# Binary cross-entropy: from three pools and casting stores to one in-place float32 ring with a clip

## Chip, cores and metric

One core of a Trainium2 chip. The metric is the device time of one execution in microseconds (us), as a median over runs. The program runs on one core alone; all runs quoted are of the state "fast". The profile shows one execution from its first to its last instruction, some 1.7 us less than the timed value.

## The reference

Two inputs of 8192 x 8192 float32 (predictions, uniform in 0.01 to 0.99, and targets, 0 or 1), one float32 output of the same shape:

```python
pred = np.clip(pred, eps, 1 - eps)                                   # eps = 1e-7
return -(target * np.log(pred) + (1 - target) * np.log(1 - pred))
```

As the targets are 0 or 1, this is `-log(|target - 1 + pred|)`: one subtraction, an absolute value (or square), one logarithm, one scaling. Each input is read once and the output written once: 805.3 MB on the HBM side.

## The kernel before

The rows are cut into 64 blocks of 128 rows, 128 partitions x 32 KiB. Targets are cast to bf16 on the way in; the result is kept as fp16 and cast back to float32 on the way out. Three pools with 3, 2 and 2 buffers carry predictions, targets and results.

```python
pool_p = ctx.enter_context(tc.tile_pool(name="bce_p", bufs=3 if big else 2))
pool_t = ctx.enter_context(tc.tile_pool(name="bce_t", bufs=2))
pool_o = ctx.enter_context(tc.tile_pool(name="bce_o", bufs=2))
# ...
def ops(bi, rows, r0, g0, t_p, t_t):
    t_o = pool_o.tile([P, F], fp16, name="t_o", tag="t_o")
    p_sl = t_p[:rows]
    nc.vector.scalar_tensor_tensor(out=p_sl, in0=p_sl, scalar=1.0, in1=t_t[:rows], op0=sub, op1=add)
    nc.scalar.activation(out=p_sl, in_=p_sl, func=Square)
    nc.scalar.activation(out=p_sl, in_=p_sl, func=Ln)
    nc.vector.tensor_scalar(out=t_o[:rows], in0=p_sl, scalar1=-0.5, scalar2=None, op0=mult)
    # ... the store of t_o is noted as pending
for bi in range(n_blk):
    # ... predictions (SyncE for block 0, else GpSimd), then targets (GpSimd), then the store of block bi-2 (GpSimd)
    # ... ops(); the last two blocks in 4 and 8 column pieces, in place in float32, stored from SyncE
```

Of the kernel before, what the change touches and what calls it, by code (L numbers as in the profile page):

```python
# [1 line left out]

# [4 lines left out]


@with_exitstack
def kernel(  # L10
    ctx: ExitStack,
    tc: tile.TileContext,
    pred: bass.AP,
    target: bass.AP,
    out: bass.AP,
):
    nc = tc.nc
    fp32 = mybir.dt.float32
    fp16 = mybir.dt.float16
    bf16 = mybir.dt.bfloat16  # L20

    P = nc.NUM_PARTITIONS

    pred_f = pred.flatten_outer_dims()
    target_f = target.flatten_outer_dims()
    out_f = out.flatten_outer_dims()

    R, C = pred_f.shape

    F = 8192 if C % 8192 == 0 else C  # L30
    n_col = C // F
    n_row = (R + P - 1) // P
    n_blk = n_row * n_col

    big = (R % P == 0) and n_blk >= 8 and F == 8192

    sub = mybir.AluOpType.subtract
    add = mybir.AluOpType.add
    mult = mybir.AluOpType.mult

    Square = mybir.ActivationFunctionType.Square
    Ln = mybir.ActivationFunctionType.Ln

    pool_p = ctx.enter_context(tc.tile_pool(name="bce_p", bufs=3 if big else 2))
    pool_t = ctx.enter_context(tc.tile_pool(name="bce_t", bufs=2))
    pool_o = ctx.enter_context(tc.tile_pool(name="bce_o", bufs=2))
    pool_w = ctx.enter_context(tc.tile_pool(name="bce_w", bufs=1))

    warm = pool_w.tile([1, 8], fp32, name="warm", tag="warm")
    nc.vector.memset(warm, 1.0)  # L50
    nc.scalar.activation(out=warm, in_=warm, func=Ln)  # L51

    lb = n_blk - 1
    slb = n_blk - 2

    pending: dict[int, list] = {}

    def emit_store(b: int, n: int | None = None):
        lst = pending[b]
        n = len(lst) if n is None else n  # L60
        for _ in range(n):
            dram, sl = lst.pop(0)
            nc.gpsimd.dma_start(out=dram, in_=sl)  # L63
        if not lst:
            del pending[b]

    def ops(bi, rows, r0, g0, t_p, t_t):
        t_o = pool_o.tile([P, F], fp16, name="t_o", tag="t_o")
        p_sl = t_p[:rows]
        nc.vector.scalar_tensor_tensor(  # L70
            out=p_sl, in0=p_sl, scalar=1.0, in1=t_t[:rows], op0=sub, op1=add
        )
        nc.scalar.activation(out=p_sl, in_=p_sl, func=Square)  # L73
        nc.scalar.activation(out=p_sl, in_=p_sl, func=Ln)  # L74
        nc.vector.tensor_scalar(  # L75
            out=t_o[:rows], in0=p_sl, scalar1=-0.5, scalar2=None, op0=mult
        )
        pending.setdefault(bi, []).append(
            (out_f[r0 : r0 + rows, g0 : g0 + F], t_o[:rows])
        )  # L80

    def ops_tail(rows, r0, g0, t_p, t_t, nchunk):
        W = F // nchunk
        for k in range(nchunk):
            c0 = k * W
            p_sl = t_p[:rows, c0 : c0 + W]
            nc.vector.scalar_tensor_tensor(  # L87
                out=p_sl,
                in0=p_sl,
                scalar=1.0,  # L90
                in1=t_t[:rows, c0 : c0 + W],
                op0=sub,
                op1=add,
            )
            nc.scalar.activation(out=p_sl, in_=p_sl, func=Square)  # L95
            nc.scalar.activation(out=p_sl, in_=p_sl, func=Ln)  # L96
            nc.vector.tensor_scalar(  # L97
                out=p_sl, in0=p_sl, scalar1=-0.5, scalar2=None, op0=mult
            )
            nc.sync.dma_start(  # L100
                out=out_f[r0 : r0 + rows, g0 + c0 : g0 + c0 + W], in_=p_sl
            )

    for bi in range(n_blk):
        i, j = divmod(bi, n_col)
        r0 = i * P
        rows = min(P, R - r0)
        g0 = j * F

        t_p = pool_p.tile([P, F], fp32, name="t_p", tag="t_p")  # L110
        t_t = pool_t.tile([P, F], bf16 if big else fp32, name="t_t", tag="t_t")

        if big and bi == 0:
            nc.sync.dma_start(out=t_p[:rows], in_=pred_f[r0 : r0 + rows, g0 : g0 + F])
        else:
            nc.gpsimd.dma_start(out=t_p[:rows], in_=pred_f[r0 : r0 + rows, g0 : g0 + F])  # L116
        nc.gpsimd.dma_start(out=t_t[:rows], in_=target_f[r0 : r0 + rows, g0 : g0 + F])  # L117

        s = bi - 2
        if s in pending:  # L120
            emit_store(s)

        if big and bi == slb:
            ops_tail(rows, r0, g0, t_p, t_t, 4)
        elif big and bi == lb:
            ops_tail(rows, r0, g0, t_p, t_t, 8)
        else:
            ops(bi, rows, r0, g0, t_p, t_t)

    for b in sorted(pending):  # L130
        emit_store(b)


# [1 line left out]
_INS = ['pred', 'target']  # L135
_OUTS = [((8192, 8192), 'float32')]


# [23 lines left out]
```

## Time and profile before

| | before |
|---|---|
| median (3 runs) | 1867.4 us (1867.38 to 1867.8) |
| span of the profile | 1865.7 us |
| Vector / Scalar busy | 45% / 48% |
| DMA engines | 9 or 10 tenths in all 40 slices |
| steady distance between blocks (600 to 1750 us) | 29.06 us |

The prediction below shows the lines and reads them.

Some measures come from the packet and landing records of the trace rather than from a printed view. A 4 MB transfer is spread over 16 DMA engines, each with eight row packets. A row packet normally takes 1.21 to 1.25 us. Each engine reports its own landing; the **landing spread** is the time from the first to the last of the 16 landings of one DMA. The **end of the last targets** is when the last packet of the last target load ends.

### The profile page before, as it was taken

To read this page: it belongs to the slowest core of one execution; us is meant where nothing else is said; L and a number is where in the kernel's file an instruction comes from. 1 tells how busy PE (TensorE), PEld (TensorE's weight loads), DVE (VectorE), ACT (ScalarE), POOL (GpSimd) and SP (SyncE) were. 2 spreads that over 40 slices of the span, in tenths; PEclk is the share of its full clock that TensorE was granted. 3 is DMA by queue.
4 is the path that set the end of the run, shared out by engine and by line. 5 is a ranking of instruction groups with operands and counts; after the bars stand their busy time and mean duration, and the time that the engine had idled before them with its cause. 6 is when DMAs were issued, how large, how long until landed. Compare 5 with 4: busy or idle time off the path is not lost.

```text
span 1865.7 us, 804 instructions
## 1 busy us (share of the span) xinstructions
DVE 841.3 (45%) x149; ACT 903.3 (48%) x150; POOL 100.9 (5%) x193
## 2 busy tenths in 40 slices
DVE  2645344453443534435344353453534535345353
ACT  3653644535445354453544635446354463553654
POOL 0000000000000000000000000000000000000000
DMA  9999999999999999999999999999999999999999
GB/s 325 338 377 353 351 379 344 375 356 347 384 341 376 356 346 387 344 368 363 343 388 345 364 369 341 390 344 360 371 343 386 344 359 372 347 379 352 352 378 351
DMA packets 29093, 671.14 MB, mean 360 GB/s; under 512 B 3232, under 2 KB 3232, under 8 KB 4256
## 3 DMA queue, kind: packets, MB, share of 16 engines
q0 software_dynamic: 27216, 658.52, 99.9%
q1 hardware_dynamic: 1872, 12.58, 1.7%
q14 instruction: 5, 0.04, 0.0%
HBM read 536.87 MB, written 268.44 MB: 432 GB/s over the span
## 4 chain that ended last, share of the span: by engine, by line
DMA 80%; issue 14%; ACT 2%; DVE 2%; another core or an unknown queue 1%; POOL 0%; POOLq 0%; DVEq 0%; PEldq 0%
DMA t_t<-in_target_dram 80%; DVE t_p L70 1%; ACT t_p L96 1%; ACT t_p L95 1%; DVE t_o L75 0%; ACT t_p L73 0%; ACT t_p L74 0%; DVE t_p L87 0%; DVE t_p L97 0%; POOL t_p L116 0%; POOL out_dram L63 0%; POOLq L117 0%; POOL t_t L117 0%; POOLq L63 0%
## 5 line engine op out<-in xcount | busy, mean ns | idle before, releaser
L73 ACT ACTIVATE t_p<-t_p 128x8192 f32<-128x8192 f32 x62 | 435.8, 7029 | 923.6 <-DVE t_p L70 923.6
L75 DVE TENSOR_SCALAR t_o<-t_p 128x8192 f16<-128x8192 f32 x62 | 274.4, 4427 | 845.0 <-ACT t_p L74 845.0
L70 DVE SCALAR_TENSOR_TENSOR t_p<-t_p,t_t 128x8192 f32<-128x8192 f32 x62 | 538.9, 8693 | 144.8 <-DMA t_t<-in_target_dram 144.8
L74 ACT ACTIVATE t_p<-t_p 128x8192 f32<-128x8192 f32 x62 | 435.8, 7029 | 2.0
L63 POOL DMA_DIRECT2D out_dram<-t_o x62 | 33.4, 538 | 1121.9 <-DVE t_o L75 1101.2
L117 POOL DMA_DIRECT2D t_t<-in_target_dram x64 | 34.1, 533 | 581.5 <-DVE t_p L70 580.7
L116 POOL DMA_DIRECT2D t_p<-in_pred_dram x63 | 33.9, 537 | 0.3 <-issue 0.3
L95 ACT ACTIVATE t_p<-t_p 128x1024 f32<-128x1024 f32 (+1 forms) x12 | 15.6, 1327 | 26.5 <-DVE t_p L87 26.5
L87 DVE SCALAR_TENSOR_TENSOR t_p<-t_p,t_t 128x1024 f32<-128x1024 f32 (+1 forms) x12 | 18.4, 1575 | 17.2 <-DMA t_t<-in_target_dram 17.2
L96 ACT ACTIVATE t_p<-t_p 128x1024 f32<-128x1024 f32 (+1 forms) x12 | 15.6, 1330 | 0.1
L97 DVE TENSOR_SCALAR t_p<-t_p 128x1024 f32<-128x1024 f32 (+1 forms) x12 | 10.3, 868 | 7.9 <-ACT t_p L96 7.9
L51 ACT ACT_TABLE_LOAD x1 | 1.3, 1283 | 0.7 <-PEq L146 0.7
L50 DVE MEMSET warm<- 1x8 f32 x1 | 0.1, 65 | 0.8 <-PEq L146 0.8
L51 ACT ACTIVATE warm<-warm 1x8 f32<-1x8 f32 x1 | 0.2, 208 | 0.0
L146 POOL MEMSET const-float32-0.0<- 128x1 f32 x1 | 0.1, 100 | 0.2 <-issue 0.2
L146 POOL MEMSET const-bfloat16-1.0<- 128x1 bf16 x1 | 0.1, 102 | 0.0
L146 POOL MEMSET const-float32-1.0<- 128x1 f32 x1 | 0.1, 100 | 0.0
L146 POOL MEMSET const-uint8-127<- 128x1 uint8 x1 | 0.1, 100 | 0.0
## 6 DMA issues: line engine op xcount, KB each, us to landing
t_p<-in_pred_dram POOLq DMA_DIRECT2D x63, 4096.0 KB, 49.3
out_dram<-t_o POOLq DMA_DIRECT2D x62, 4096.0 KB, 40.1
t_t<-in_target_dram POOLq DMA_DIRECT2D x64, 2048.0 KB, 49.0
t_p<-in_pred_dram SPq DMA_DIRECT2D x1, 4096.0 KB, 19.6
out_dram<-t_p SPq DMA_DIRECT2D x4, 1024.0 KB, 27.3
out_dram<-t_p SPq DMA_DIRECT2D x8, 512.0 KB, 8.5
```

The source lines that it names most:

```text
L51: nc.scalar.activation(out=warm, in_=warm, func=Ln)
L63: nc.gpsimd.dma_start(out=dram, in_=sl)
L70: nc.vector.scalar_tensor_tensor(out=p_sl, in0=p_sl, scalar=1.0, in1=t_t[:rows], op0=sub, op1=add)
L73: nc.scalar.activation(out=p_sl, in_=p_sl, func=Square)
L74: nc.scalar.activation(out=p_sl, in_=p_sl, func=Ln)
L75: nc.vector.tensor_scalar(out=t_o[:rows], in0=p_sl, scalar1=-0.5, scalar2=None, op0=mult)
L87: nc.vector.scalar_tensor_tensor(out=p_sl, in0=p_sl, scalar=1.0, in1=t_t[:rows, c0 : c0 + W], op0=sub, op1=add,)
L95: nc.scalar.activation(out=p_sl, in_=p_sl, func=Square)
L96: nc.scalar.activation(out=p_sl, in_=p_sl, func=Ln)
L97: nc.vector.tensor_scalar(out=p_sl, in0=p_sl, scalar1=-0.5, scalar2=None, op0=mult)
L116: nc.gpsimd.dma_start(out=t_p[:rows], in_=pred_f[r0 : r0 + rows, g0 : g0 + F])
L117: nc.gpsimd.dma_start(out=t_t[:rows], in_=target_f[r0 : r0 + rows, g0 : g0 + F])
```

## The change

The stated intent: one ring of four 32 KiB slots for predictions, worked in place in float32 to the end, and a matching ring of targets; a clip as in the reference; and one GpSimd queue in the order store, predictions, targets, so that a load waits for a store issued one block earlier. The diff is condensed; cuts are marked.

```diff
-    pool_p (3 buffers), pool_t (2), pool_o (2)                  [cut]
+    ring_p = pool.tile([P, SLOTS * W], fp32, ...)               # SLOTS = 4, W = 8192
+    ring_t = pool.tile([P, SLOTS * W], bf16, ...)
-        t_o = pool_o.tile([P, F], fp16, ...)                    # result in fp16, casting store
+    def clip(k, ...):   tensor_scalar(out=p, in0=p, scalar1=EPS, scalar2=1 - EPS, max, min)
+    def front(k, ...):  scalar_tensor_tensor(out=p, in0=t, scalar=1.0, in1=p, subtract, add)
+                        activation(out=p, in_=p, func=Act.Abs)   # was Square
+                        activation(out=p, in_=p, func=Act.Ln)
+    def back(k, ...):   tensor_scalar(out=p, in0=p, scalar1=-1.0, mult)   # was -0.5, to fp16
+        for k in range(SLOTS):
+            load(k)
+        clip(0)
+        front(0)
+        for k in range(1, n - 1):
+            clip(k)
+            front(k)
+            back(k - 1)
+            store(k - 1)                                         # plain float32
+            if k >= 2 and k - 2 + SLOTS < n:
+                load(k - 2 + SLOTS)                              # slot of block k-2
+        back(n - 2)
+        store(n - 2)                                             # last two blocks: SyncE
+        clip(n - 1)                                              # then half, quarter, quarter
+        [cut: front, back and two half-width stores of the last block]
```

More of the change, by code (lines that the diff above doesn't have):

```diff
@@ L4 @@
 import concourse.tile as tile
-from concourse import bass_utils, mybir
+from concourse import mybir
 from concourse._compat import with_exitstack
+EPS = 1e-7
+W = 8192
+SLOTS = 4
 @with_exitstack
@@ L18 @@
     fp32 = mybir.dt.float32
-    fp16 = mybir.dt.float16
     bf16 = mybir.dt.bfloat16
+    Alu = mybir.AluOpType
+    Act = mybir.ActivationFunctionType
     P = nc.NUM_PARTITIONS
-    pred_f = pred.flatten_outer_dims()
-    target_f = target.flatten_outer_dims()
-    out_f = out.flatten_outer_dims()
-    R, C = pred_f.shape
-    F = 8192 if C % 8192 == 0 else C
-    n_col = C // F
-    n_row = (R + P - 1) // P
-    n_blk = n_row * n_col
-    big = (R % P == 0) and n_blk >= 8 and F == 8192
-    sub = mybir.AluOpType.subtract
@@ L38 @@
-    add = mybir.AluOpType.add
-    mult = mybir.AluOpType.mult
-    Square = mybir.ActivationFunctionType.Square
-    Ln = mybir.ActivationFunctionType.Ln
-    pool_p = ctx.enter_context(tc.tile_pool(name="bce_p", bufs=3 if big else 2))
-    pool_t = ctx.enter_context(tc.tile_pool(name="bce_t", bufs=2))
-    pool_o = ctx.enter_context(tc.tile_pool(name="bce_o", bufs=2))
-    pool_w = ctx.enter_context(tc.tile_pool(name="bce_w", bufs=1))
-    warm = pool_w.tile([1, 8], fp32, name="warm", tag="warm")
@@ L50 @@
-    nc.vector.memset(warm, 1.0)
-    nc.scalar.activation(out=warm, in_=warm, func=Ln)
-    lb = n_blk - 1
-    slb = n_blk - 2
-    pending: dict[int, list] = {}
-    def emit_store(b: int, n: int | None = None):
-        lst = pending[b]
-        n = len(lst) if n is None else n
-        for _ in range(n):
-            dram, sl = lst.pop(0)
-            nc.gpsimd.dma_start(out=dram, in_=sl)
-        if not lst:
-            del pending[b]
-    def ops(bi, rows, r0, g0, t_p, t_t):
-        t_o = pool_o.tile([P, F], fp16, name="t_o", tag="t_o")
-        p_sl = t_p[:rows]
+    R, C = pred.shape
@@ new lines, with chunks @@
+    n = R * C // (P * W)
+    assert n * P * W == R * C and n > SLOTS
+    def chunks(ap):
+        return ap.rearrange("r c -> (r c)").rearrange("(k p w) -> k p w", p=P, w=W)
+    pred_c, target_c, out_c = chunks(pred), chunks(target), chunks(out)
+    pool = ctx.enter_context(tc.tile_pool(name="rings", bufs=1))
+    ring_p = pool.tile([P, SLOTS * W], fp32, name="ring_p", tag="ring_p")
+    ring_t = pool.tile([P, SLOTS * W], bf16, name="ring_t", tag="ring_t")
+    warm = pool.tile([1, 8], fp32, name="warm", tag="warm")
@@ new lines, in slot, with load, store, clip @@
+    def slot(ring, k, off=0, w=W):
+        c = k % SLOTS * W + off
+        return ring[:, c : c + w]
+    def load(k):
+        queue = nc.sync if k == 0 else nc.gpsimd
+        queue.dma_start(out=slot(ring_p, k), in_=pred_c[k])
+        nc.gpsimd.dma_start(out=slot(ring_t, k), in_=target_c[k])
+    def store(k, off=0, w=W):
+        queue = nc.sync if k >= n - 2 else nc.gpsimd
+        queue.dma_start(out=out_c[k, :, off : off + w], in_=slot(ring_p, k, off, w))
+    def clip(k, off=0, w=W):
+        p = slot(ring_p, k, off, w)
+        nc.vector.tensor_scalar(
+            out=p, in0=p, scalar1=EPS, scalar2=1 - EPS, op0=Alu.max, op1=Alu.min
+        )
@@ L70, in ops, with front @@
+    def front(k, off=0, w=W):
+        p, t = slot(ring_p, k, off, w), slot(ring_t, k, off, w)
         nc.vector.scalar_tensor_tensor(
-            out=p_sl, in0=p_sl, scalar=1.0, in1=t_t[:rows], op0=sub, op1=add
+            out=p, in0=t, scalar=1.0, in1=p, op0=Alu.subtract, op1=Alu.add
         )
-        nc.scalar.activation(out=p_sl, in_=p_sl, func=Square)
-        nc.scalar.activation(out=p_sl, in_=p_sl, func=Ln)
-        nc.vector.tensor_scalar(
-            out=t_o[:rows], in0=p_sl, scalar1=-0.5, scalar2=None, op0=mult
-        )
@@ L78, in ops @@
-        pending.setdefault(bi, []).append(
-            (out_f[r0 : r0 + rows, g0 : g0 + F], t_o[:rows])
-        )
-    def ops_tail(rows, r0, g0, t_p, t_t, nchunk):
-        W = F // nchunk
-        for k in range(nchunk):
-            c0 = k * W
-            p_sl = t_p[:rows, c0 : c0 + W]
-            nc.vector.scalar_tensor_tensor(
-                out=p_sl,
-                in0=p_sl,
-                scalar=1.0,
-                in1=t_t[:rows, c0 : c0 + W],
-                op0=sub,
-                op1=add,
-            )
-            nc.scalar.activation(out=p_sl, in_=p_sl, func=Square)
-            nc.scalar.activation(out=p_sl, in_=p_sl, func=Ln)
-            nc.vector.tensor_scalar(
-                out=p_sl, in0=p_sl, scalar1=-0.5, scalar2=None, op0=mult
-            )
-            nc.sync.dma_start(
-                out=out_f[r0 : r0 + rows, g0 + c0 : g0 + c0 + W], in_=p_sl
-            )
@@ L104 @@
-    for bi in range(n_blk):
-        i, j = divmod(bi, n_col)
-        r0 = i * P
-        rows = min(P, R - r0)
-        g0 = j * F
-        t_p = pool_p.tile([P, F], fp32, name="t_p", tag="t_p")
-        t_t = pool_t.tile([P, F], bf16 if big else fp32, name="t_t", tag="t_t")
-        if big and bi == 0:
-            nc.sync.dma_start(out=t_p[:rows], in_=pred_f[r0 : r0 + rows, g0 : g0 + F])
-        else:
-            nc.gpsimd.dma_start(out=t_p[:rows], in_=pred_f[r0 : r0 + rows, g0 : g0 + F])
-        nc.gpsimd.dma_start(out=t_t[:rows], in_=target_f[r0 : r0 + rows, g0 : g0 + F])
-        s = bi - 2
-        if s in pending:
-            emit_store(s)
-        if big and bi == slb:
-            ops_tail(rows, r0, g0, t_p, t_t, 4)
-        elif big and bi == lb:
-            ops_tail(rows, r0, g0, t_p, t_t, 8)
-        else:
-            ops(bi, rows, r0, g0, t_p, t_t)
@@ L130, with back @@
-    for b in sorted(pending):
-        emit_store(b)
+        nc.scalar.activation(out=p, in_=p, func=Act.Abs)
+        nc.scalar.activation(out=p, in_=p, func=Act.Ln)
+    def back(k, off=0, w=W):
+        p = slot(ring_p, k, off, w)
+        nc.vector.tensor_scalar(out=p, in0=p, scalar1=-1.0, scalar2=None, op0=Alu.mult)
+    with tc.manual_schedule():
+        for k in range(SLOTS):
+            load(k)
+        nc.vector.memset(warm, 1.0)
+        nc.scalar.activation(out=warm, in_=warm, func=Act.Ln)
+        clip(0)
[9 more added lines that the diff above has]
+        store(n - 2)
+        h, q = W // 2, W // 4
+        clip(n - 1)
+        front(n - 1, 0, h)
+        front(n - 1, h, q)
+        back(n - 1, 0, h)
+        store(n - 1, 0, h)
+        front(n - 1, h + q, q)
+        back(n - 1, h, q)
+        back(n - 1, h + q, q)
+        store(n - 1, h, h)
```

## The prediction

> **What bounds the kernel now.** I start with the page's totals, because they say whether an engine or the transfers set the time.
>
> ```profile
> span 1865.7 us, 804 instructions
> DVE 841.3 (45%) x149; ACT 903.3 (48%) x150; POOL 100.9 (5%) x193
> DMA  9999999999999999999999999999999999999999
> q0 software_dynamic: 27216, 658.52, 99.9%
> HBM read 536.87 MB, written 268.44 MB: 432 GB/s over the span
> ```
>
> No compute engine is busy half the time, while the DMA engines are full in every slice and the GpSimd queue alone accounts for 99.9% of their time. The last line is the important one: 536.87 + 268.44 = 805.3 MB cross the HBM side, three transfers of 4.19 MB for each of 64 blocks. A target transfer lands as 2 MB of bf16 but is read as 4 MB of float32.
>
> Second view: how one block runs in the steady state, in order of time (start, duration, engine, line, wait before it).
>
> ```profile
> 903.15 0.54 POOL L63 DMA_DIRECT2D out_dram<-t_o  x1 [18.05 <-DVE t_o L75]
> 903.68 0.54 POOL L116 DMA_DIRECT2D t_p<-in_pred_dram  x1
> 904.73 8.69 DVE L70 SCALAR_TENSOR_TENSOR t_p<-t_p,t_t 128x8192 f32<-128x8192 f32 x1 [1.87 <-DMA t_t<-in_target_dram]
> 913.46 7.03 ACT L73 ACTIVATE t_p<-t_p 128x8192 f32<-128x8192 f32 x1 [15.06 <-DVE t_p L70]
> 913.72 0.53 POOL L117 DMA_DIRECT2D t_t<-in_target_dram  x1 [9.50 <-DVE t_p L70]
> 920.51 7.03 ACT L74 ACTIVATE t_p<-t_p 128x8192 f32<-128x8192 f32 x1
> 927.58 4.43 DVE L75 TENSOR_SCALAR t_o<-t_p 128x8192 f16<-128x8192 f32 x1 [14.15 <-ACT t_p L74]
> 933.74 8.69 DVE L70 SCALAR_TENSOR_TENSOR t_p<-t_p,t_t 128x8192 f32<-128x8192 f32 x1 [1.74 <-DMA t_t<-in_target_dram]
> ```
>
> Two successive L70 start at 904.73 and 933.74, 29.01 us apart; over many blocks I get 29.05. In that period Vector works 13.1 us and Scalar 14.1 us. 12.58 MB in 29.05 us is 433 GB/s.
>
> Third view: the issues, with the time from issue to landing.
>
> ```profile
> t_p<-in_pred_dram POOLq DMA_DIRECT2D x63, 4096.0 KB, 49.3
> out_dram<-t_o POOLq DMA_DIRECT2D x62, 4096.0 KB, 40.1
> t_t<-in_target_dram POOLq DMA_DIRECT2D x64, 2048.0 KB, 49.0
> ```
>
> A transfer needs about 29.05 / 3 = 9.68 us of the DMA engines, yet it lands 40 to 49 us after issue: four or five stand in line. So the chain of waits, which repeats "target DMA 49 us, then 9 us" (a two-buffer wait), describes the line, not a latency that could be removed. The packet records confirm it. In the steady state the target phase lasts 9.65 us, the store phase 9.68 us and the prediction phase 9.71 us, although two of these cast and one does not. The casts therefore cost no rate now.
>
> **What the Trainium skill says.** "DMA: Bandwidth & Descriptors", section "Where 436 GB/s comes from", puts the ceiling of the 16 DMA engines at 435.2 GB/s. This trace's 433 is within 0.5% of it, so by an estimate from that page 805.3 MB cannot take less than 1850.5 us, and all that any reordering can save is 15 us (0.8%). The same page's "SWDGE vs HWDGE vs iDMA" says that a casting transfer has to be issued from GpSimd. That is why target loads stay there; the float32 stores no longer have to. "SBUF — State Buffer", section "Who interferes with whom", warns that tensor_scalar in Vector's two-port mode blocks GpSimd, which writes the descriptors of its own DMAs. L75's 4.43 us for 8192 elements is 1.85 elements per ns against 0.94 for L70, which fits a two-port mode. In this trace the GpSimd issues last 0.53 to 0.54 us and are placed after L75 ends, so it shows no block.
>
> **The change, part by part.** Traffic: the same 64 loads of predictions, 64 of targets and 64 stores of 4 MB at the HBM side. The store's source is now 4 MB of float32 in place of 2 MB of fp16, but the phases above are equal whichever side is smaller. Expected 9.68 us each, 192 x 9.68 = 1859 us of DMA work as before.
>
> Vector: the new clip is a one-source float32 operation like L75, so 4.43 us; 64 of them add 283 us. The other two keep 8.69 and 4.43. Vector becomes 64 x 17.55 = 1123 us, 60% of the span. Scalar: Abs replaces Square, one pass each, 7.03 us assumed; one table load as before (the built program has one). Scalar stays at 900 us. Both lie beside the transfers, and the clip only needs the predictions, which land one transfer (9.7 us) before the targets, so it is done before the targets come.
>
> Order: call T the landing of block k's targets. Vector runs the subtraction to T+8.7 and then the negation of block k-1, whose logarithm ended long before, to T+13.1. GpSimd then issues store k-1, and loads for k+2, which wait for store k-2 to land. That store went just behind targets k in the line and lands near T+9.7 plus 0.4 (the delay from last packet to waiting instruction that the trace shows), about T+10.1, earlier than the T+13.1 at which GpSimd gets there. In the line at T stand store k-2 and two loads, 29 us of work; at T+13.1 still 16 us. So the line is shorter than now, but never empty. At the start the four slots put eight loads, 77 us, in the line. Store 0 goes behind them by 55 us, and load 4 waits for it to land, near 91 us, while store 1 is still queued until 100 us: 8 us of margin.
>
> Tail: in the kernel before, packets of the last targets end at 1838.7 us, of which about 4.7 us are packets of store 62 that cut in (248 of its 512 had started). Without them they would end at E = 1834.0, and the new kernel does not cut in before that: store 62 is issued about 1.8 us before the targets land (Scalar finishes block 62 at T+22.8, negation to T+27.2, next landing at T+29.05), plus 1.0 us from a SyncE issue to the first packet, as at the start of this trace. After E stand stores 61 and 62, until E+19.4. Landing is E+0.4. From the landing: clip 63 ends at 2.6, half a subtraction at 7.0, Abs and Ln of a half at 14.0, negation at 16.3: the first half store arrives before E+19.4 and leaves no hole, and ends at E+24.2. The last quarter: subtraction to 18.5, Abs and Ln to 22.1, negation to 23.3; its store starts packets at about E+24.7, a hole of some 0.5 us, with 4.84 us of data and up to 0.6 us of filling: E+30.1 = 1864.1. Now the last packets end at 1864.0, after 4 and 8 KiB rows that cost 159 ns where an eighth of a 32 KiB row's 1213 is 152. The two tails cancel: a hole of about 1 us against half a microsecond of small rows. The span ends 1.7 us after the last packet, giving 1865.8, and the timed run is 1.7 us above the span (1867.4 against 1865.7): **1867.5**. I round to 1867.
>
> **Rivals.** A dry line: if GpSimd's single queue put loads behind a late store, the engines would idle every block. For it: three issues in one queue now wait for each other, and Vector has 34% more to do. Against: the 16 us worked out above. If it happened at 1 us a block, the time would be 1930. Second, blocked descriptors: more two-port Vector time. Clip and issue would have to coincide, but the next predictions land near T+19.4 and the issues are at T+13.1. Even a block of 4.4 us is below the 16 us in line, so it too is hidden; if my margin is wrong, the same 1930 or more. Third, cheaper plain stores: packet durations are 1243 ns for casting stores and 1213 for plain prediction loads. If that 30 ns were rate, eight packets per engine and 62 blocks give 15 us, the whole room under the ceiling, and 1853. Against: the phases differ by 0.03 us the other way. The fourth is a bound by Vector at 1123 us, which is far off.
>
> **Range and chances.** The DMA work has nowhere to go but up to the ceiling (-12 us) or to small holes at start or end (+9 us): 1859 to 1876. Over 2% faster would need 1830, below the estimated ceiling: 0.005. Over 2% slower needs a hole of 0.6 us in every block: 0.025. Within 2%: 0.97.
>
> **What would show it.** Right: DMA full in all slices, one block per 29.0 to 29.1 us, Vector near 1123 us with clips of 4.4 us, stores landing near 26 us after issue in place of 40 (16 in line and 9.7 of their own), prediction loads near 36 and target loads near 45 in place of 49. Wrong: DMA slices below 9 in the middle, subtraction starts more than 29.3 us apart, store phases other than 9.7 us, GpSimd issues much longer than 0.54 us, or a last packet more than 3 us off 1864.

## The result, and the profile after

| | before | after |
|---|---|---|
| median (4 runs each) | 1867.5 us (1867.38 to 1867.8) | 1871.14 us (1870.88 to 1871.25) |
| span of the profile | 1865.7 us | 1869.4 us |
| Vector / Scalar busy | 45% / 48% | 60% / 48% |

The ratio is 1.0019, 95% interval 1.0005 to 1.0033 (ratios are the mean time of one kernel's fast runs over that of the other's of the same rounds, so not quite the ratio of the medians quoted). Within 2%, and inside the predicted range; 4 us above the predicted 1867. Since the runs of each of these two kernels scatter by 0.4 us, these 4 us are worth an explanation.

First the page of the changed kernel, the lines that answer to those of before:

```profile
span 1869.4 us, 755 instructions
DVE 1117.4 (60%) x197; ACT 902.2 (48%) x134; POOL 110.6 (6%) x193
DMA  9999999999999999999999999999999999999998
q0 software_dynamic: 27216, 658.52, 98.8%
```

Still full, except the last slice (an 8): a little is lost at the very end. The GpSimd queue's share is 98.8% where it was 99.9%, but most of that is no loss: the packets of plain stores are shorter in the records (median 1213 ns against 1245 for casting stores; eight a store and 62 stores make 16 us per engine, 0.9% of the span), and the blocks come no faster for it. The steady block in order of time (start, duration, engine, line, wait):

```profile
791.94 8.69 DVE L73 SCALAR_TENSOR_TENSOR ring_p<-ring_t,ring_p 128x8192 f32<-128x8192 bf16 x1 [5.30 <-DMA ring_t<-in_target_dram]
800.55 4.42 DVE L81 TENSOR_SCALAR ring_p<-ring_p 128x8192 f32<-128x8192 f32 x1
805.26 0.54 POOL L63 DMA_DIRECT2D out_dram<-ring_p  x1 [27.46 <-DVE ring_p L81]
805.79 0.54 POOL L58 DMA_DIRECT2D ring_p<-in_pred_dram  x1
806.31 0.55 POOL L59 DMA_DIRECT2D ring_t<-in_target_dram  x1
811.26 4.43 DVE L67 TENSOR_SCALAR ring_p<-ring_p 128x8192 f32<-128x8192 f32 x1 [6.29 <-DMA ring_p<-in_pred_dram]
821.01 8.69 DVE L73 SCALAR_TENSOR_TENSOR ring_p<-ring_t,ring_p 128x8192 f32<-128x8192 bf16 x1 [5.33 <-DMA ring_t<-in_target_dram]
```

The order is the predicted one: subtraction at T, negation after it, store and loads at T+13.3, the clip when the next predictions land and before their targets do. The blocks are 29.07 us apart (791.94 to 821.01). The issues of the changed kernel, with the time to landing at the end of each line:

```profile
ring_p<-in_pred_dram POOLq DMA_DIRECT2D x63, 4096.0 KB, 34.5
out_dram<-ring_p POOLq DMA_DIRECT2D x62, 4096.0 KB, 25.3
ring_t<-in_target_dram POOLq DMA_DIRECT2D x64, 2048.0 KB, 43.6
```

Predicted were 36, 26 and 45: the line of transfers is shorter, and never empty.

Where, then, are the 4 us? The steady distance is nearly the same, so I looked at single stretches. The next two lines are the answers for the subtraction of the kernel before and of the changed one between 190 and 490 us: count, durations in ns, first and last start.

```profile
L70 DVE SCALAR_TENSOR_TENSOR t_p<-t_p,t_t x10: 8691/8693/8694, 207.4 to 469.1; 128x8192 f32<-128x8192 f32 x10
```

```profile
L73 DVE SCALAR_TENSOR_TENSOR ring_p<-ring_t,ring_p x10: 8691/8692/8693, 208.2 to 472.5; 128x8192 f32<-128x8192 bf16 x10
```

Nine distances: (469.1 - 207.4) / 9 = 29.08 us before, (472.5 - 208.2) / 9 = 29.37 us after. The changed kernel loses 0.3 us per block here and no longer later: between 900 and 1200 us the same view gives 29.06 and 29.08. The landing records show the form of the loss. The **landing spread** is the time from the first to the last of the 16 landings of one DMA; it says how far the engines have drifted out of step. The landing spread of the changed kernel is 0.56 us at 91 us, 1.19 at 247, 2.40 at 326, 3.49 at 404, 3.89 at 482, and then stays (4.2 at the end); the kernel before goes from 0.6 to 1.6 in the whole run. And the packet records show where (I call a row packet over 1.30 us **stretched**): between 100 and 530 us there are 68 stretched packets against 2, and 66 of the 68 are packets of target loads, most of them the last packet that an engine has before it turns to a store. Some engines are thus held back at the switch from load to store, block after block, until they are out of step. A subtraction starts 0.1 us after the last of the 16 landings that it waits for, so the slowest engine sets the time: the last targets end at 1837.5 us where the prediction put 1834.0.

### The profile page after: what moved, and what is told of

Read it like the earlier page. It is cut to its first block, busy times and chain, and to the rows that moved or that the text cites. A ratio compares the mean times of both kernels' runs of the same rounds, so it can differ in the third digit from the quotient of the medians.

```text
span 1869.4 us, 755 instructions
## 1 busy us (share of the span) xinstructions
DVE 1117.4 (60%) x197; ACT 902.2 (48%) x134; POOL 110.6 (6%) x193
## 3 DMA queue, kind: packets, MB, share of 16 engines
q0 software_dynamic: 27216, 658.52, 98.8%
## 4 chain that ended last, share of the span: by engine, by line
issue 86%; DMA 6%; POOL 5%; DVE 2%; ACT 1%; POOLq 0%; DVEq 0%; PEldq 0%
DMA ring_t<-in_target_dram 4%; DMA out_dram<-ring_p 2%; POOL ring_t L59 2%; POOL out_dram L63 2%; POOL ring_p L58 1%; DVE ring_p L73 1%; ACT ring_p L76 1%; ACT ring_p L77 1%; DVE ring_p L81 1%; DVE ring_p L67 0%; POOLq L58 0%; DVEq L73 0%; PEldq L136 0%; POOLq L63 0%
## 5 line engine op out<-in xcount | busy, mean ns | idle before, releaser
L76 ACT ACTIVATE ring_p<-ring_p 128x8192 f32<-128x8192 f32 (+1 forms) x66 | 450.4, 6824 | 955.6 <-DVE ring_p L73 955.6
L73 DVE SCALAR_TENSOR_TENSOR ring_p<-ring_t,ring_p 128x8192 f32<-128x8192 bf16 (+1 forms) x66 | 556.5, 8433 | 325.1 <-DMA ring_t<-in_target_dram 325.0
L67 DVE TENSOR_SCALAR ring_p<-ring_p 128x8192 f32<-128x8192 f32 x64 | 283.3, 4426 | 400.9 <-DMA ring_p<-in_pred_dram 400.9
L77 ACT ACTIVATE ring_p<-ring_p 128x8192 f32<-128x8192 f32 (+1 forms) x66 | 450.4, 6824 | 2.1
L81 DVE TENSOR_SCALAR ring_p<-ring_p 128x8192 f32<-128x8192 f32 (+1 forms) x66 | 283.1, 4290 | 17.7 <-ACT ring_p L77 17.7
L63 POOL DMA_DIRECT2D out_dram<-ring_p x62 | 40.8, 658 | 1692.7 <-DVE ring_p L81 1662.7
L58 POOL DMA_DIRECT2D ring_p<-in_pred_dram x63 | 36.1, 573 | 18.4 <-DMA out_dram<-ring_p 18.1
L59 POOL DMA_DIRECT2D ring_t<-in_target_dram x64 | 35.3, 552 | 0.8 <-PEq L136 0.8
## 6 DMA issues: line engine op xcount, KB each, us to landing
ring_p<-in_pred_dram POOLq DMA_DIRECT2D x63, 4096.0 KB, 34.5
out_dram<-ring_p POOLq DMA_DIRECT2D x62, 4096.0 KB, 25.3
ring_t<-in_target_dram POOLq DMA_DIRECT2D x64, 2048.0 KB, 43.6
```

The costliest lines, as they stand in the source:

```text
L58: queue.dma_start(out=slot(ring_p, k), in_=pred_c[k])
L59: nc.gpsimd.dma_start(out=slot(ring_t, k), in_=target_c[k])
L63: queue.dma_start(out=out_c[k, :, off : off + w], in_=slot(ring_p, k, off, w))
L67: nc.vector.tensor_scalar(out=p, in0=p, scalar1=EPS, scalar2=1 - EPS, op0=Alu.max, op1=Alu.min)
L73: nc.vector.scalar_tensor_tensor(out=p, in0=t, scalar=1.0, in1=p, op0=Alu.subtract, op1=Alu.add)
L76: nc.scalar.activation(out=p, in_=p, func=Act.Abs)
```

## Experiments

Two theories were in play. **A**: it is the stores, plain float32 in place of casting fp16. **B**: it is the new order and the shorter line. To these come the tail, the clip, and the blocked issues of rival two. In the table, "stretched" counts packets over 1.30 us between 100 and 1800 us (each run has four to eight instruction fetches in this stretch; in the kernel before, with five fetches, the five stretched packets stand right beside them).

| run | median us (range) | last targets end | last packet ends | stretched | spread near 1720 us |
|---|---|---|---|---|---|
| before | 1867.5 (1867.4 to 1867.8) | 1838.7* | 1864.0 | 5 | 1.6 |
| after | 1871.1 (1870.9 to 1871.3) | 1837.5 | 1867.8 | 70 | 4.2 |
| e1_before_f32_out | 1874.5 (1873.5 to 1874.7) | 1845.8* | 1871.0 | 96 | 7.9 |
| e2_after_cast_store | 1868.1 (1868.0 to 1868.3) | 1834.5 | 1864.8 | 3 | 1.6 |
| e3_after_no_clip | 1871.5 (1868.8 to 1871.9) | 1838.5 | 1867.6 | 56 | 5.5 |
| e4_after_clip_early | 1870.4 (1869.3 to 1873.1) | 1837.2 | 1866.3 | 84 | 3.8 |
| e5_after_targets_first | 1875.6 (1874.0 to 1878.4) | 1839.1, predictions\*\* | 1873.5 | 66 | 5.7 |
| e6_cast_store_clip_early | 1867.0 (1866.5 to 1867.3) | 1834.6 | 1863.7 | 3 | 1.7 |
| e7_after_stores_on_sp | 1879.4 (1879.3 to 1882.0) | 1841.0 | 1878.6 | 13 | 6.8 |
| e8_after_vector_beside_issue | 1872.2 (1872.0 to 1876.7) | 1838.3 | 1868.6 | 36 | 5.2 |
| e9_after_store_halves | 1875.9 (1874.3 to 1876.3) | 1842.1\*\* | 1872.1 | 81 | 6.0 |
| e11_cast_store_first_16 | 1872.0 (1871.5 to 1872.4) | 1838.3 | 1868.7 | 57 | 5.3 |
| e10_after_three_slots | 2866.4 (2 runs) | 2835.1 | 2862.9 | 992 | 0.6 |

\* with packets of the second-last block's stores mixed in. \*\* the last of the 16 landings, some 0.3 us after the last packet. In the rounds of the experiments, the kernel before had medians of 1867.57 to 1867.68; the changed kernel was timed in its first session alone (four runs). Except for e10, no ratio to the kernel before is over 1.0063: what follows is about differences of a few us, read against the scatter of the runs.

In the changed kernel and e2 to e4, e6, e8 and e11, which load in the same order, the end of the last targets follows the spread: 1834.5 us at a spread of 1.6, 1837.2 at 3.8, 1837.5 at 4.2, 1838.3 at 5.2, 1838.5 at 5.5. The number of stretched packets alone says less. In e10, whose line runs dry in every block, 992 packets are stretched, but on nearly all engines at once, and the spread stays under 0.9 us.

### 1. Plain stores in the kernel before (e1)

```diff
-        t_o = pool_o.tile([P, F], fp16, name="t_o", tag="t_o")
+        t_o = pool_o.tile([P, F], fp32, name="t_o", tag="t_o")
```

> The kernel before with its out tile in float32 (two buffers of 32 KiB), so that all stores are plain and nothing else moves. Theory A (a plain float32 store right behind a casting target load stretches the last target packets of the early blocks, until the 16 DMA engines have drifted apart): slow last target packets (over 1.25 us) come back in several early blocks, the spread of the 16 landings of one DMA grows from 0.6 to some 4 us by 500 us, and the time rises by 2 to 4 us to about 1870. Rival B (the drift comes from the new order and the shorter line of transfers): time within 0.7 us of before (1867.5), landing spread as before, 0.6 to 1.6 us.

Measured: 1874.5 us, ratio 1.0036 (1.0024 to 1.0049). This one word costs 6.9 us, more than theory A had said, and rival B falls. The page of this kernel shows that nothing else moved, neither the compute nor the depth of the line (40.2 and 49.0 us to landing, as before), while the last slice drops:

```profile
span 1872.7 us, 804 instructions
DVE 841.3 (45%) x149; ACT 903.3 (48%) x150; POOL 100.5 (5%) x193
DMA  9999999999999999999999999999999999999998
q0 software_dynamic: 27216, 658.52, 98.7%
out_dram<-t_o POOLq DMA_DIRECT2D x62, 4096.0 KB, 40.2
t_t<-in_target_dram POOLq DMA_DIRECT2D x64, 2048.0 KB, 49.0
```

### 2. Casting stores in the changed kernel (e2)

```diff
-    ring_t = pool.tile([P, SLOTS * W], bf16, name="ring_t", tag="ring_t")
+    ring_t = pool.tile([P, SLOTS * W], fp16, name="ring_t", tag="ring_t")
     # store:
+        ring = ring_p if k >= n - 2 else ring_t
     # back:
+        o = p if k >= n - 2 else slot(ring_t, k, off, w)
```

> The changed kernel with the negation writing fp16 into the used target slot and the 62 GpSimd stores casting back to float32, order and rings unchanged; the last two blocks stay float32 on SyncE. Theory A: no slow last target packets after the first store, landing spread stays 0.6 to 1.6 us, last targets land near 1834.5 instead of 1837.9, time 1867 to 1868.5, that is 3 us below the changed kernel (1871.1). Rival B: time and drift as in the changed kernel, 1870.5 to 1871.5.

Measured: 1868.1 us, 3.1 below the changed kernel; the runs agree within 0.3 us. The last targets end at 1834.5, as the prediction had put it (1834.0). Order, rings and depth are those of the changed kernel, so theory A is shown from both sides: give the kernel before plain stores and it drifts, give the changed kernel casting stores and it does not. (That e2 also loads its targets as fp16 in place of bf16 is not what keeps it in step: e11 below does the same and drifts once its stores are plain.) Its subtractions in the same stretch, 190 to 490 us, are back at (469.2 - 207.5) / 9 = 29.08 us:

```profile
L74 DVE SCALAR_TENSOR_TENSOR ring_p<-ring_t,ring_p x10: 8691/8692/8693, 207.5 to 469.2; 128x8192 f32<-128x8192 f16 x10
```

### 3. No clip (e3), and the last clip earlier (e4)

```diff
 e3: all 64 calls of clip() removed
 e4:
+        clip(n - 1)
         back(n - 2)
         store(n - 2)
-        clip(n - 1)
```

> The changed kernel without its 64 clips (the draw lies within 0.01 to 0.99, so the result stays right). My theory: the clip is off the path in all blocks but the last, where it stands 4.4 us in front of the last subtraction: Vector falls from 1117 to about 834 us, the three long GpSimd issues at 55, 75 and 92 us (4.17, 4.16 and 2.98 us) become 0.54 us, the time falls by 1 to 2 us at the tail only (1869 to 1870). Rival (clips block descriptor writes or feed the drift): the drift goes too and the time falls by 4 us or more, to 1867 or less.

> The changed kernel with the last block's clip moved in front of the negation of the block before it, so that it runs before the last targets land. My theory: the end of the changed kernel is set by the compute chain of the last block, not by the line of transfers; the chain gets 4.4 us shorter, the hole before the last store closes, and 1 to 2 us are saved: 1869 to 1870, the same as without any clip. Rival (the end is set by the transfers alone, the hole costs nothing): within 0.4 us of the changed kernel, 1870.8 to 1871.5.

Measured: 1871.5 and 1870.4 us. Both miss their expected 1869 to 1870, and by their times alone they are inconclusive: kernels that drift scatter by several us from run to run (e4: 1869.26 to 1873.05). The traces tell more. From the end of the last targets to the last packet takes 1867.8 - 1837.5 = 30.3 us in the changed kernel, but 29.1 us in e3 and in e4; 29.05 would be three transfers without a hole. The packet records show the hole: in the changed kernel all 16 engines are idle from 1861.73 to 1862.76, before the last half store; e2, e8 and e11 have the same hole of 1.0 us, and e3, e4 and e6 have none. So the last clip does cost 1.2 us, and where the drift ended in that run hides it. All other clips are free: Vector fell from 1117.4 to 834.5 us in e3, and the drift stayed (spread 5.5 us). Of the three long GpSimd issues at the start two became 0.54 us and one stayed at 2.98 us (below).

### 4. Both repairs together (e6)

The diffs of e2 and e4 in one kernel.

> The changed kernel with casting fp16 stores (as in the second run) and the last clip moved ahead (as in the fourth). My theory: without drift the shorter compute chain at the end is seen clean: 1.2 us below the 1868.1 of the casting stores alone, 1866.7 to 1867.1, a little below the kernel before (1867.6), with little scatter between runs (0.3 us). Rival (the tail gain of the fourth run was drift luck): 1868.0 to 1868.3.

Measured: 1867.0 us, 1.1 below e2, as expected, with the runs within 0.7 us (a little more than the 0.3 expected). Four lines of its tail, in order of time, show the shorter chain: the subtraction of the last block starts when its targets land, with the clip done before, where in the changed kernel it started at 1840.50 behind a clip of 1836.05.

```profile
1825.31 4.43 DVE L68 TENSOR_SCALAR ring_p<-ring_p 128x8192 f32<-128x8192 f32 x1 [6.32 <-DMA ring_p<-in_pred_dram]
1829.65 4.42 DVE L83 TENSOR_SCALAR ring_p<-ring_p 128x8192 f32<-128x8192 f32 x1
1835.00 6.63 DVE L74 SCALAR_TENSOR_TENSOR ring_p<-ring_t,ring_p 128x4096 f32<-128x4096 f16 x2 [0.93 <-DMA ring_t<-in_target_dram]
...
1855.17 1.23 DVE L83 TENSOR_SCALAR ring_p<-ring_p 128x2048 f32<-128x2048 f32 x1 [2.78 <-ACT ring_p L78]
```

The ratio to the kernel before is 0.9996 (0.9984 to 1.0009): the same. The full reference's clip is in it, so it is the version I would keep, but not for its time.

### 5. What kind of switch? (e5, e9, e11, e7)

In e5 each block loads its targets first, so that a plain prediction load stands before each store:

```diff
-        queue.dma_start(out=slot(ring_p, k), in_=pred_c[k])
         nc.gpsimd.dma_start(out=slot(ring_t, k), in_=target_c[k])
+        queue.dma_start(out=slot(ring_p, k), in_=pred_c[k])
```

> The changed kernel with each block's targets loaded in front of its predictions, so that in the line a plain prediction load, not a casting target load, stands right before each plain store. Theory A1 (the switch from a casting load to a plain store makes the engines drift): after the start no stretched packets, landing spread of one DMA stays 0.5 to 1.6 us, the last prediction lands near 1834.5 us. Theory A2 (any load followed by a plain store does it): stretched prediction packets in the early blocks, spread grows to 3 to 8 us, last landing 1837 or later. The tail is 4.4 us longer in both, since the clip now stands behind the landing: time about 1872 under A1, 1875 or more under A2.

Measured: A2. The stretched packets move with the order: of the targets none is stretched between 100 and 600 us, now it is the last prediction packets (1.3 to 2.0 us), and the spread grows to 5.7 us. So the load need not cast. The landing records also give the last landing of the predictions, 1839.1 us, as A2 had it (1837 or later).

In e9 each store in the loop is cut into two half-width plain stores:

```diff
-            store(k - 1)
+            store(k - 1, 0, W // 2)
+            store(k - 1, W // 2, W // 2)
```

> The changed kernel with each of the 61 plain stores inside the loop cut into two half-width plain stores (16 KiB rows in SBUF, as a casting store reads them, in place of 32 KiB). Theory P1 (the drift belongs to plain stores whatever their row size): stretched packets and a landing spread of 3 to 8 us again, time 1871 to 1875. Theory P2 (it is the 32 KiB read from SBUF per packet): no drift, spread 0.5 to 1.7 us, time 1868 to 1869 (some 0.5 us for the extra rows).

Measured: P1. The spread grows to 6.0 us and the time is 1875.9 us (just over the expected range). The size of the row in SBUF is not what matters.

In e11 blocks 0 to 15 have casting stores, the others plain ones:

```diff
+        ring = ring_p if k >= 16 else ring_t          # and the same in back()
```

> The changed kernel with casting stores for blocks 0 to 15 and plain stores from block 16 on. Theory L (the drift starts whenever plain stores meet engines that are in step): no stretched packets before some 530 us, then about a dozen blocks with them, landing spread from 0.5 to 4 us or more by 1000 us, time as the changed kernel, 1870 to 1874. Theory S (it belongs to the start of the program): no drift at all, 1868.0 to 1868.5.

Measured: L. One stretched packet between 100 and 530 us, then 56; the spread is 0.70 us at 479 us, 3.1 at 636, 4.4 at 870; the time is 1872.0 us, 0.9 above that of the changed kernel. The drift is not a matter of the program's start. It begins when plain stores meet engines that are in step, and in the runs here it slowed or stopped by itself once they were some 3 to 8 us apart, by 500 us in the changed kernel, but only by some 1300 in e3.

In e7 all stores are issued from SyncE and no longer stand in one line with the loads:

```diff
-        queue = nc.sync if k >= n - 2 else nc.gpsimd
+        queue = nc.sync
```

> The changed kernel with all stores issued from SyncE, plain float32, so that they no longer stand in the GpSimd line but share the engines with the loads packet by packet. Theory A1 (drift comes from casting load followed by plain store in one line): store and load packets now mix all the time, so stretched packets either vanish or show up everywhere; if they vanish, spread under 1.6 us and time 1867 to 1869. Rival (the mixing of plain stores with casting loads itself stretches packets): over 1876. No strong view; I lean to the first, with a store landing in about 19 us instead of 25.

Measured: 1879.4 us, so the lean was wrong, although stretched packets are few (13); a store landed 23.2 us after issue, not 19. The trace is of the slowest of the five runs (1882.0 us). In it the spread swings between 1 and 7 us with the block, the distance between subtractions swings too, and the last targets end 3.5 us later than in the changed kernel. The larger part of the loss is at the end: 37.6 us lie between the last targets and the last packet in place of 30.3. The last block's subtraction starts at 1851.23 us in place of 1840.50, while the two stores before it have landed by 1858.3 (1857.2 in the changed kernel). So the line runs dry: all 16 engines are idle from 1857.9 to 1866.1 and from 1871.2 to 1873.5 us, 10.5 us in place of 1.0. In the stretches below, the last two numbers are the DMA share and GB/s:

```profile
1842.00:1858.00 16.00, 15.39 (x4) 2.71 (x2) 0.00 (x0) 1.00 0.80 345
1858.00:1866.00 8.00, 3.01 (x2) 7.93 (x4) 0.00 (x0) 1.00 0.00 0
1866.00:1878.00 12.00, 3.85 (x3) 4.52 (x3) 0.00 (x0) 1.00 0.83 350
```

This run therefore says little about plain stores as such; why the loads land so unevenly when stores mix with them is not settled by it.

### 6. Blocked issues (e8)

The start of the changed kernel shows rival two of the prediction at work, three times in all. GpSimd's issue of the first store stands beside a clip, and a later load issue beside a negation:

```profile
55.24 4.42 DVE L67 TENSOR_SCALAR ring_p<-ring_p 128x8192 f32<-128x8192 f32 x1
55.62 4.17 POOL L63 DMA_DIRECT2D out_dram<-ring_p  x1 [50.54 <-DVE ring_p L81]
...
90.03 4.42 DVE L81 TENSOR_SCALAR ring_p<-ring_p 128x8192 f32<-128x8192 f32 x1
...
91.59 2.98 POOL L58 DMA_DIRECT2D ring_p<-in_pred_dram  x1 [12.51 <-DMA out_dram<-ring_p]
```

The issue at 55.62 ends at 59.79, 0.13 us after the clip (59.66); that at 91.59 ends at 94.57, 0.12 us after the negation (94.45). An issue of 0.54 us has become one of 4.17. This agrees with what the Trainium skill says in "SBUF — State Buffer", section "A bandwidth-pool intuition that's wrong (but worth ruling out)": blocked until the Vector operation ends, plus about 115 ns. To see what it would cost in every block, e8 puts useless two-port operations beside every issue:

```diff
             store(k - 1)
+            for _ in range(6):   # dummy: 128 x 2048 float32
+                nc.vector.tensor_scalar(out=dummy, in0=dummy, scalar1=EPS, scalar2=1 - EPS, op0=Alu.max, op1=Alu.min)
```

> The changed kernel with six useless two-port Vector operations of 2048 elements (about 1.2 us each, 7 us together) right behind each negation, that is beside the three GpSimd issues of each block. My theory: the issues are blocked (the block's three take several us instead of 1.6), but 16 us of transfers stand in the line, so the time stays at that of the changed kernel, 1870 to 1873. Rival (a block of the issue reaches the DMA engines): 1 us or more per block, 1930 or more.

Measured: 1872.2 us, with two runs of five at 1874.7 and 1876.7. The three issues of a block now take 3.5 us (0.96 + 1.27 + 1.27) in place of 1.6, less than I had thought; presumably the gaps between the short operations let them through (not tested):

```profile
DVE 1564.7 (84%) x570; ACT 902.3 (48%) x134; POOL 213.4 (11%) x193
...
804.32 0.96 POOL L64 DMA_DIRECT2D out_dram<-ring_p  x1 [25.56 <-DVE ring_p L82]
805.27 1.27 POOL L59 DMA_DIRECT2D ring_p<-in_pred_dram  x1
806.53 1.27 POOL L60 DMA_DIRECT2D ring_t<-in_target_dram  x1
```

Two us of block against 16 us in the line: nothing reaches the transfers, even with Vector at 84%.

### 7. Three slots (e10)

```diff
-SLOTS = 4
+SLOTS = 3
```

> The changed kernel with rings of three slots, so that each load waits for the store issued one iteration earlier and stands behind the newest store. By the working of the prediction, 9.7 us of transfers stand in the line when the targets land and the next issue comes 13.1 us later, so the line runs dry every block: store, load, load (29.05 us) start only 13.1 us and about 1 us of issue after the landing, 43 us per block and 2700 to 2800 us in all. Rival (the DMA engines stay full with three slots): below 1900.

Measured: 2866 us, ratio 1.53. The mechanism is as expected, the size was under: 45.28 us per block in place of 43. The DMA row of the page, two successive subtractions and the store's issue between them show it:

```profile
DMA  9757566575766757576675756657576675756657
...
1012.99 8.69 DVE L73 SCALAR_TENSOR_TENSOR ring_p<-ring_t,ring_p 128x8192 f32<-128x8192 bf16 x1 [5.27 <-DMA ring_t<-in_target_dram]
1026.31 0.54 POOL L63 DMA_DIRECT2D out_dram<-ring_p  x1 [43.68 <-DVE ring_p L81]
...
1058.27 8.69 DVE L73 SCALAR_TENSOR_TENSOR ring_p<-ring_t,ring_p 128x8192 f32<-128x8192 bf16 x1 [5.27 <-DMA ring_t<-in_target_dram]
```

The issue comes 13.32 us after the landing, and the next landing 45.28 - 13.32 = 31.96 us after the issue: 29.05 of transfer and 2.9 of starting up and landing, where I had put 1. The prediction's "shorter, but never empty" was thus a matter of one slot. The spread is 0.3 to 0.8 us all along: engines that wait for the same issue start together again (in the block above within 0.2 us of each other, at 1027.4). The changed kernel shows this once, at its only hole: the spread is 4.2 us before it and 0.2 us at the last store, behind it.

## Why the prediction was right, and where it was 4 us off

- **The bound.** Right. The DMA engines stay full; 283 us more of Vector work cost nothing but the last clip's 1.2 us.
- **The line.** Right. Landings of 25.3, 34.5 and 43.6 us after issue, issues at T+13.3, no dry moment. The fourth slot carries this (e10).
- **The start.** Right in effect: the first load that waits for a store was issued at 91.59 (predicted near 91). Three issues took up to 4.2 us there. The prediction had ruled out blocked issues for the steady state and had not looked at the start; the margin hid them.
- **The tail.** Right in size: E to the last packet 30.1 us predicted, 30.3 measured, and the hole of 0.5 to 1 us was real (all engines idle for 1.0 us; worth 1.2 us by e4 and e6).
- **The DMA work.** This step failed: "Expected 9.68 us each, 192 x 9.68 = 1859 us of DMA work as before", and with it E = 1834.0. In steady state it holds (29.06 us before, 29.05 after, from 600 to 1750 us), but in a dozen early blocks the plain stores hold back some engines, and E became 1837.5. That is 3.5 us over the prediction's E and 3.0 us over that of e2 (1834.5), where the drift is taken out; in time it is 3.1 us (1871.1 against 1868.1 for e2).
- **The third rival** (plain stores are cheaper by 30 ns a packet). The packets did get shorter (medians of 1213 ns against 1245), and nothing came of it: the argument from phases held, though its 0.03 us are too fine to be read (taken from landings instead of first packets, the phases shift by up to 0.1 us). What the plain store does to the loads beside it had the other sign.
- **Its signs of being wrong.** Three of those that it named came true although the time lay in the range: subtraction starts 29.37 us apart on the mean between 190 and 490 us (it named 29.3), GpSimd issues of 4.17 us (0.54), and a last packet 3.8 us off 1864 (3). The first and the last are the drift; the second cost nothing. The DMA slices in the middle stayed at 9.
- **The range.** 1859 is not what its own sum gives: 1867 less 12 is 1855. The measured time lies on the other side, so nothing hangs on it.

The sum of the parts: drift 3.1 us (after minus e2), hole of the last clip 1.1 us (e2 minus e6), and the rest of the change -0.6 us (e6 at 1867.0 minus before at 1867.6, which the interval of that ratio does not set apart from 0), together 3.6 us. Kernels that drift scatter by up to 5 us between runs (e8), so 3.1 us is the drift of this kernel in its own session and no constant: e8 and e11, which drift too, were at 1872.2 and 1872.0.

Open: what inside the chip holds an engine back at the switch, why a casting store does so only at the first switch (31 stretched target packets in e2 between 77 and 80 us, none of targets after 100), and why the drift stops. The runs narrow it to plain stores following any load, in a line that is never empty, on engines that are in step.

## What to carry to other kernels

With the DMA engines full, the changes of the compute were worth nothing here but at the tail, and three things counted: that the line never runs empty, how it ends, and whether the 16 engines stay in step. Work out for each load what it waits for and how much is left in the line at that moment: 16 us were enough here to hide blocked issues and 34% more Vector work, and one slot fewer cost 53%. A store that casts was not slower than a plain one here, and replacing it lost 3 to 7 us; look at the spread of one DMA's landings before taking shorter packets for a gain.

## What the Trainium skill lacked or had wrong

- "DMA: Bandwidth & Descriptors" has nothing on DMA engines drifting apart in a mixed stream. Here plain float32 stores behind loads took the landing spread of one DMA from 0.6 us to between 4 and 8, within some 500 us in these two kernels and more slowly in others, and cost 3.1 us (changed kernel) or 6.9 us (kernel before); casting stores left it at 1.6 to 1.8 us.
- The same page, section "SWDGE vs HWDGE vs iDMA", says who has to issue a cast, not what it costs. Here it cost no rate: the phases of casting load, casting store and plain load were 9.65, 9.68 and 9.71 us.
- The same page, "Issuing engines are not separate DMA queues", says that issuing from several engines saves only the time of the issue; it does not say what the new interleaving can do to the order. Here moving the stores to SyncE was not neutral: 1879.4 us against 1871.1, as the loads landed unevenly and the line ran dry for 10.5 us at the end.
- The same page, "Anatomy of one DMA — SWDGE (gpsimd) path", gives some 2 us fixed cost per DMA. In a line that is never empty none of it shows: 9.68 us per 4.19 MB, 0.04 above the 9.64 that its ceiling of 435.2 GB/s gives. In the line that ran dry (e10) 2.9 us showed per block.
- No page that I found says what an instruction fetch does to a running stream of data; what is said of fetches is about the instructions. Each run had five to eight of them (8 KiB packets), and in the kernel before a row packet right beside each of the five took 1.3 to 1.6 us in place of 1.21 to 1.25.
